# A batched matrix product in 32-row groups: which engine waits for the stores at the end

## The chip, the cores and the metric

The kernel runs on one core of one Trainium2 chip. A core has a matrix engine (TensorE, PE in the profile), a vector engine (VectorE, DVE), a scalar engine (ScalarE, ACT), a general engine (GpSimd, POOL) and an engine that issues transfers and waits (SyncE, SP). Each has its own stream of instructions; they meet only at semaphores. Transfers between the chip's main memory and the on-chip memory are done by 16 DMA engines. The metric is the time of one execution on the device in microseconds (us); less is better.

## The reference

```python
x: float32 [32, 256, 512]      # batch, i, j
y: float32 [32, 512, 384]      # batch, j, k
out = np.einsum('bij,bjk->bik', x, y).astype(np.float32)   # [32, 256, 384]
```

For each of 32 batches, a 256 x 512 matrix times a 512 x 384 matrix. 41.94 MB are read and 12.58 MB written.

## The kernel before, in words

The work is cut into N = 8 steps of Q = 4 batches. The 128 partitions of the on-chip memory are four groups of 32, one batch to a group. In a step each partition holds 8 rows of x (`x_sb`, 2,048 KB for the step) and 16 rows of y (`y_sb`, 3,072 KB), both double-buffered.

The engines share a step like this:

- SyncE issues all transfers, on one queue. It loads y and x of the first two steps ahead of everything else; later loads wait until GpSimd has cast the tile that they overwrite (L98 to L102). Then it issues three stores by `store` (L93 to L96): steps 0 to 4 together, steps 5 and 6 together, and step 7. Each store raises semaphore `s_out` by 16 when it has landed.
- GpSimd casts x and y from float32 to float16 (`round_x`, L121; `round_y`, L130).
- VectorE transposes x in 32 x 32 blocks, two float16 numbers at a time (`transpose_x`, L156), so that j comes to lie on the partitions.
- TensorE forms the products, in 16 slices of j with 32 rows each, the four batches side by side in the array (L217), and sums them in the accumulators `o_ps`.
- ScalarE copies 11 and VectorE 5 of every 16 blocks of the accumulators to `o_sb`, which holds the whole output (`collect`, L165).

The order on each engine is the order in which the program is written; semaphores hold it. SyncE's end is L107 to L111: it waits until ScalarE and VectorE have copied the last blocks, issues the last store, raises `s_sp` by 1, and then waits at L111 until `s_out` has reached 48, that is until all three stores have landed, and subtracts 48 so that the next execution starts from zero. Raising `s_sp` tells GpSimd that SyncE has no more waits on any other semaphore. GpSimd, whose casts are long done, waits for that (L144) and then clears the 24 semaphores of the kernel in one instruction (L145). `s_out` is the one semaphore that stands outside the cleared range; it has the next number, 123, and the range ends with `s_sp`, 122.

Of the kernel before, what the change touches and what calls it, by code (L numbers as in the profile page):

```python
# [19 lines left out]
def kernel(  # L20
# [41 lines left out]
    s_out = nc.alloc_semaphore("s_out")  # L62
# [28 lines left out]
    sp = nc.sync  # L91
# [16 lines left out]
    sp.wait_ge(s_dve, NE)  # L108
    store(N - 1, N)
    sp.sem_inc(s_sp, 1)  # L110
    sp.wait_op(s_out, 16 * 3, "sem-ge").then_inc(s_out, -16 * 3)  # L111

# [4 lines left out]
    po = nc.gpsimd  # L119
# [23 lines left out]
        round_y(n)  # L143
    po.wait_ge(s_sp, 1)  # L144
    po.sem_clear(range(nums[0], nums[-1] + 1))  # L145

# [132 lines left out]
```

## Time and profile before

| | |
|---|---|
| time, median of 3 runs | 132.00 us (131.89 to 132.18) |
| profiled execution | 132.13 us |
| its span, first to last instruction of the kernel | 130.8 us |
| busy: TensorE, VectorE, ScalarE, GpSimd | 61.4, 82.7, 84.1, 74.2 us |
| DMA queue, share of 16 engines | 98.1% |
| landing of the three stores after their issue | 33.9, 17.3, 11.5 us |

The span is shorter than the time of the same execution, because the time holds more than the kernel's own instructions. In the page, "L111" is line 111 of the kernel, a queue name with a q (SPq, POOLq) is an engine's sequencer, which waits, branches and issues without the engine counting as busy, and "a <- b" in a list of waits says that a waited for b. Rows of groups give the number of instructions after an x, and the duration in ns as least, median and most. A row of the timeline begins with the start and the length in us.

### The profile page before, as it was taken

What the parts mean: (1) busy time and instruction counts of PE and PEld (TensorE: products, weight loads), DVE (VectorE), ACT (ScalarE), POOL (GpSimd) and SP (SyncE); (2) the same over time, 40 slices, a digit from 0 to 9 for tenths busy, and PEclk for the clock granted to TensorE, in tenths of its full rate; (3) what the DMA queues carried; (4) which work ended last, traced back from release to release, by engine and by line L of the source; (5) the groups of instructions that cost most, each with busy time, mean ns of one, the idle gap of its engine ahead of it and who ended that gap; (6) DMA issues with size and microseconds to landing.
All of it is one profiled execution on the core that took longest, in us unless ns stands there. A gap on an engine that the chain in (4) does not pass through costs nothing. (4 is left out here: it accounts for less than half of the span.)

```text
span 130.8 us, 3199 instructions
## 1 busy us (share of the span) xinstructions
PE 61.4 (47%) x1024; PEld 46.7 (36%) x1024; DVE 82.7 (63%) x144; ACT 84.1 (64%) x178; POOL 74.2 (57%) x42
## 2 busy tenths in 40 slices
PE   0000009910992589089329905980975499100000
PEld 0000009800991566046129604970953236000000
DVE  0000036899379999985997997599999957920000
ACT  0400000599659989993998899399999957994000
POOL 0006991199929965992899459758973970000000
PEclk9999999995589689977986985599599959965555
DMA  5999999999999999999999999999999999999995
GB/s 120 451 396 441 421 431 451 443 408 428 451 413 421 438 443 401 436 436 443 423 458 398 443 408 466 398 418 436 463 398 408 427 438 425 436 428 421 425 440 248
DMA packets 3379, 54.55 MB, mean 417 GB/s; under 512 B 304, under 2 KB 304, under 8 KB 304
## 3 DMA queue, kind: packets, MB, share of 16 engines
q1 hardware_dynamic: 3376, 54.53, 98.1%
q14 instruction: 3, 0.02, 0.0%
HBM read 41.94 MB, written 12.58 MB: 417 GB/s over the span
## 5 line engine op out<-in xcount | busy, mean ns | idle before, releaser
L165 ACT COPY o_sb<-o_ps (+1 forms) x176 | 82.6, 469 | 31.7 <-PE o_ps L217 29.6
L217 PE MATMUL o_ps<-y_r,xt_sb 32*128 32x384 f16 x1024 | 61.4, 384 | 50.4 <-PEq L214 49.5
L217 PEld LDWEIGHTS o_ps<-y_r,xt_sb 32*128 32x128 f16 x1024 | 46.7, 107 | 64.6 <-issue 56.8
L156 DVE STREAM_TRANSPOSE xt_sb<-x_r 128x256 f32<-128x256 f32 x64 | 38.1, 626 | 30.9 <-POOL x_r L126 18.4
L136 POOL CAST y_r<-y_sb 128x1536 f16<-128x1536 f32 (+1 forms) x22 | 44.3, 2049 | 15.8 <-DMA y_sb<-in_y_dram 15.3
L165 DVE COPY o_sb<-o_ps 32x384 f32 (+1 forms) x80 | 44.6, 557 | 1.6
L126 POOL CAST x_r<-x_sb 128x2048 f16<-128x2048 f32 x16 | 30.2, 1893 | 16.8 <-DVE o_sb L165 12.1
L202 ACT ACT_TABLE_LOAD x1 | 1.3, 1283 | 3.4 <-PEq L78 3.4
L265 POOL MEMSET const-float32-0.0<- 128x1 f32 x1 | 0.1, 98 | 0.2 <-issue 0.2
L202 ACT COPY spare<-const-float32-0.0 1x1 f32<-1x1 f32 x1 | 0.2, 190 | 0.0
L265 POOL MEMSET const-bfloat16-1.0<- 128x1 bf16 x1 | 0.1, 101 | 0.0
L265 POOL MEMSET const-uint8-127<- 128x1 uint8 x1 | 0.1, 101 | 0.0
L265 POOL MEMSET const-float32-1.0<- 128x1 f32 x1 | 0.1, 98 | 0.0
## 6 DMA issues: line engine op xcount, KB each, us to landing
y_sb<-in_y_dram SPq DMA_DIRECT2D x8, 3072.0 KB, 16.8
x_sb<-in_x_dram SPq DMA_DIRECT2D x8, 2048.0 KB, 17.0
out_dram<-o_sb SPq DMA_DIRECT2D x1, 7680.0 KB, 33.9
out_dram<-o_sb SPq DMA_DIRECT2D x1, 3072.0 KB, 17.3
out_dram<-o_sb SPq DMA_DIRECT2D x1, 1536.0 KB, 11.5
```

The lines of the kernel that those rows point to most:

```text
L126: po.tensor_copy(x_r[:, e], x_sb[n % 2][:, e * H : (e + 1) * H]).then_inc(s_cast, 1)
L136: ins = po.tensor_copy(y_r[:, s], y_sb[n % 2][:, s])
L156: v.transpose(xt_w[:, w], words[:, e, w]).then_inc(s_xt, 1)
L165: ins = copy(o_sb[g * PQ : (g + 1) * PQ, n, e, h], o_ps[h * PQ : (h + 1) * PQ, e * Q + g, :K],)
L202: a_.copy(spare, nc.const_aps.tensor(0.0, [1, 1], F32))
L217: return te.add_instruction(mybir.InstMatmult(name=nc.get_next_instruction_name(), start_tensor_calc=start, stop_tensor_calc=stop, tile_si ...
L265: nc = _bacc.Bacc("TRN2", target_bir_lowering=False, num_devices=1)
```

## The change

The last instruction of SyncE, the wait for the three stores with its subtraction, is taken from SyncE's stream and put at the end of GpSimd's stream, behind the clear. SyncE's last instruction is then the raising of `s_sp`. Everything else is the same.

```diff
     sp.wait_ge(s_dve, NE)
     store(N - 1, N)
     sp.sem_inc(s_sp, 1)
-    sp.wait_op(s_out, 16 * 3, "sem-ge").then_inc(s_out, -16 * 3)
...
     po.wait_ge(s_sp, 1)
     po.sem_clear(range(nums[0], nums[-1] + 1))
+    po.wait_op(s_out, 16 * 3, "sem-ge").then_inc(s_out, -16 * 3)
```

## The prediction

> **What bounds the kernel now.** I read the page first, the slices in time and the DMA queue before anything else, because the edit touches nothing but the waiting for transfers.
>
> ```profile
> span 130.8 us, 3199 instructions
> PE 61.4 (47%) x1024; PEld 46.7 (36%) x1024; DVE 82.7 (63%) x144; ACT 84.1 (64%) x178; POOL 74.2 (57%) x42
> DMA  5999999999999999999999999999999999999995
> q1 hardware_dynamic: 3376, 54.53, 98.1%
> ```
>
> No engine is busy for two thirds of the span, while the 16 DMA engines are busy in every slice and for 98.1% of it. The kernel is a stream of 54.53 MB on SyncE's queue with all computing under it. Neither the bytes nor the moments at which a transfer is issued are changed, so the only stretch in which the edit can act is the end. That end stands in the stage table (columns: stretch, its length, each engine's busy time and instructions, clock, DMA share, GB/s), the waits of SyncE's queue, and the timeline of the last microseconds.
>
> ```profile
> core 0: us, PE busy (x) PEld busy (x) DVE busy (x) ACT busy (x) POOL busy (x), PEclk, DMA share, GB/s
> 112.00:119.90 7.90, 0.00 (x0) 0.00 (x0) 3.09 (x6) 7.06 (x16) 0.00 (x0) 0.70 1.01 431
> 119.90:130.80 10.90, 0.00 (x0) 0.00 (x0) 0.00 (x0) 0.00 (x0) 0.00 (x0) 0.50 0.87 373
> ...
> SPq L111 <- SPq L111: 11.1, 1, 11.1
> ...
> 109.44 5.73 DVE L165 COPY o_sb<-o_ps 32x384 f32<-32x384 f32 x10
> ...
> 117.82 1.43 ACT L165 COPY o_sb<-o_ps 32x384 f32<-32x384 f32 x3
> 119.27 0.34 SPq L96 DMA_DIRECT2D out_dram<-o_sb  x1
> ...
> L145 POOLq EVENT_SEMAPHORE_RANGE_CLEAR  x1: 163/163/163, 119.7 to 119.7; - x1
> L111 SPq EVENT_SEMAPHORE  x1: 17/17/17, 130.8 to 130.8; - x1
> ```
>
> TensorE is done before 112.0, VectorE at 109.44 + 5.73 = 115.17, ScalarE at 117.82 + 1.43 = 119.25. SyncE issues the last store at 119.27, GpSimd clears semaphores at 119.7, and from 119.9 on nothing runs but the stores. SyncE waits 11.1 us for them at L111 and its 17 ns at 130.8 are the end of the span.
>
> **What lies behind the span.** The profiled execution took 132.13 us, the span is 130.8, so 1.33 us lie around it. No view shows instructions there, but the trace also records the time of each update of each semaphore, and these go on. Semaphore 2 belongs to no instruction of this kernel. Its updates, and three others on which I draw, from that record (not a view; us from the span's start):
>
> ```
> semaphore 2, ahead of the span:  -0.371 -0.337 -0.298 -0.254 -0.231 -0.119 -0.081 -0.047 0.000
> semaphore 2, end of the kernel:  111.912 119.360 120.402 120.446 130.937 130.981 131.020 131.054 131.101
> semaphore 2, after the clears:   131.895 131.929 131.967 132.011 132.035 132.133 132.171 132.206 132.252
> semaphore 123 (s_out):           last arrival 130.767, subtracted by SyncE 130.801
> semaphore 96 (start of program): last arrivals 2.893 and 3.221, subtracted by GpSimd 2.942 and 3.270
> semaphore 97 (start of program): raised by GpSimd 3.021, subtracted by SyncE 3.055
> semaphore 122 (s_sp):            cleared by GpSimd 119.838 (the last of its range)
> ```
>
> It always comes in groups of nine: a chain through five engines and back. The group at the end tells the order, set beside the ends above: 111.912 is TensorE, 119.360 ScalarE (0.11 behind its last copy), 120.402 GpSimd, 120.446 VectorE (long done, so only 0.044 behind the one ahead), 130.937 SyncE, and then four steps back through the same engines to 131.101. From 131.063 to 131.671 nearly all semaphores of the core are reset, and the third group follows. So every engine passes the chain after its last instruction of the kernel, and whoever comes last holds it up.
>
> **The change, part by part.** (1) Removed: SyncE's wait and subtraction. Nothing is queued behind it on SyncE, and no instruction of the kernel waits for SyncE after s_sp. SyncE is then done at about 119.7 and is ready in the chain 11 us early. Gain by itself: the end no longer holds SyncE's wake-up (130.767 to 130.801, 0.034) and its way into the chain (130.801 to 130.937, 0.136).
>
> (2) Added: the same wait, one instruction, on GpSimd, behind the range clear. It moves past no DMA: GpSimd issues none, and SyncE's three stores are all issued before. Nothing is queued behind it. The clear stays at 119.7, covered by the stores as now; were that cover gone it would cost its 163 ns. The instruction itself is priced by the barriers at the start of the program, where both engines execute the same kind:
>
> ```profile
> L78 POOLq EVENT_SEMAPHORE  x4: 17/17/17, 2.9 to 3.3; - x4
> L78 SPq EVENT_SEMAPHORE  x2: 17/17/17, 3.0 to 3.4; - x2
> L78 POOLq DRAIN  x2: 34/38/41, 0.7 to 3.1; - x2
> L78 SPq DRAIN  x3: 7/7/123, 2.7 to 3.1; - x3
> L265 POOLq DRAIN  x1: 188/188/188, 0.3 to 0.3; - x1
> ```
>
> 17 ns on both. From arrival to subtraction GpSimd took 49 ns (2.893 to 2.942, and 3.221 to 3.270), SyncE 34 (3.021 to 3.055, and the same at the end). So GpSimd subtracts at 130.767 + 0.049 = 130.816, 15 ns later than SyncE does now.
>
> (3) GpSimd's way from its last instruction into the chain. It starts at 119.7 with 163 ns, by the record's finer times until 119.865, and the chain shows it at 120.402: 0.537 us. No other engine needed that: ScalarE 0.11, SyncE 0.136. Today it lies under 10 us of stores and costs nothing; after the edit it is the last thing on the path. What it consists of, no row shows. It could belong to the range clear (a tail of that instruction), and then it stays covered, because the clear still runs at 119.7. It could belong to GpSimd's leaving the kernel, and then it moves to the end. Two things in the record favour the second. In the reset after the chain the last clear of semaphores 105 to 154, by the order of the engines GpSimd's share, is at 131.444, and GpSimd had no delay in the group that follows: its step at 131.967 is 0.038 behind ScalarE's, as in the group ahead of the span (0.039). It was thus ready at most 0.485 after a clear, against 0.564 (119.838 to 120.402) at the kernel's end. And TensorE, which resets last (131.671), is back in the chain 0.224 later, so a reset need not have a tail of half a microsecond. I take 0.537. Lower end: 0.11, ScalarE's; 0 is excluded by the fastest engine seen. Upper end: 0.537 + 0.188, the longest GpSimd drain in the rows.
>
> (4) GpSimd's place in the chain. SyncE is the turning point: after its step four more follow, 131.101 - 130.937 = 0.164. GpSimd is third, so six follow: 0.298 in the group ahead of the span (-0.298 to 0.000), 0.285 in the last. VectorE and SyncE are ready by then and add only their steps. I take 0.298.
>
> **The sum**, from the last arrival at 130.767. Before: 0.034 + 0.136 + 0.164 = 0.334, the chain closes at 131.101. After: 0.049 + 0.537 + 0.298 = 0.884, it closes at 131.651. Difference +0.550 us. The reset and the last group follow the closing, so I carry the difference over in full: the profiled execution would take 132.13 + 0.55 = 132.68. It stands 0.13 above the median of the runs, 132.00, so I forecast 132.55 us, 0.42% slower. With the ends of (3): 0.049 + 0.11 + 0.298 - 0.334 = +0.12, and 0.55 + 0.188 = +0.74.
>
> A measurement of this kernel can tell about 0.2%, 0.26 us, from no change; its three runs span 131.89 to 132.18.
>
> **Rivals.** *Only the place counts.* GpSimd leaves the kernel like the others, the 0.537 was the clear's tail. For it: the clear is the only kind of instruction in the kernel's end that no other engine executes; against it: the 0.485 above. With SyncE's 0.136 the sum is 0.049 + 0.136 + 0.298 - 0.334 = +0.15, with ScalarE's 0.11 it is +0.12: 132.12 to 132.15, not to be told from no change.
>
> The Trainium skill, Runtime: NRT & Kernel Launch, in its section on the preamble and postamble, describes this chain as a serpentine over five engines with 44 ns a hop, eight hops in about 355 ns. The trace agrees: 131.895 to 132.252 is 0.357. By that rule alone an engine that comes last costs by its place only, and as an estimate two more hops make 0.088 us, a time of 132.09. It has no term for an engine that is slow to leave, and that term is what decides here.
>
> *Faster.* SyncE leaves the kernel 11.1 us early (its row above), and whatever SyncE does for its own queue at the end would be done under the stores. Place: from 130.801 on, and in what follows the third group, which nothing shows. Of the visible part only 0.034 + 0.136 can go, and the same steps of GpSimd take its place; with GpSimd's six steps at 0.298 the closing would be earlier only if its wake-up and leaving together took under 0.334 - 0.298 = 0.036, less than its wake-up alone. For a gain beyond 0.26 the hidden part would have to hold some 0.4 us of SyncE's own work against the +0.12 that is left at the least: 131.7. The 1.33 around the span leave room for that, no row speaks for it.
>
> *The edit does not reach the time.* If the end of the measured time is not tied to this chain (it is taken at the span's end, plus something fixed), only the 15 ns of wake-up remain: 132.02.
>
> **How the numbers follow.** Slow leaving moved to the end, 132.55: 0.65. Only the place, 132.12 to 132.15: 0.23. Not in the measured time, 132.02: 0.07. Faster, 131.7: 0.05. So slower 0.65, the same 0.30, faster 0.05. The likeliest case has 132.35 to 132.80 for itself: its upper end of +0.74 and the spread of the runs, and below it a leaving partly owed to the clear. The range for 8 in 10 takes in the place-only case and reaches from 132.0 to 132.8; the faster case and half of the one at 132.02 lie beneath it.
>
> **What would show it.** The span should grow by no more than 0.02: GpSimd's subtraction with 17 ns at 130.8 in place of SyncE's, the 11.1 us of waiting gone from L111, the clear still at 119.7, the three stores issued and landing as before. In the record of semaphore 2, SyncE no longer makes the late step: the third update, GpSimd's, comes some 0.54 behind its subtraction, and six steps in 0.3 us follow. A third update only 0.11 to 0.15 behind the subtraction proves the first rival right. The prediction is wrong as a whole if the time moves by over 0.3 us while the chain closes as early as before, or if a store's landing moves.

## The result, and the profile after

The changed kernel takes 132.51 us (median of 6 runs, 132.41 to 132.65); the kernel before took 131.97 in its 6 runs (131.83 to 132.18). The ratio is 1.0038, with a 95% interval of 1.0028 to 1.0048: 0.5 us slower, a small change but one clear of the spread of the runs.

The page of the changed kernel, its DMA lines, two windows at the end (columns: stretch, its length, each engine's busy time and instructions, clock, DMA share, GB/s), all waits of SyncE's queue, and the rows of GpSimd's last two lines and of SyncE's last store:

```profile
span 130.6 us, 3199 instructions
DMA  5999999999999999999999999999999999999996
q1 hardware_dynamic: 3376, 54.53, 98.3%
...
112.00:119.50 7.50, 0.00 (x0) 0.00 (x0) 2.68 (x5) 6.67 (x15) 0.00 (x0) 0.84 1.00 426
119.50:130.60 11.10, 0.00 (x0) 0.00 (x0) 0.00 (x0) 0.00 (x0) 0.00 (x0) 0.50 0.90 384
...
SPq L73 <- POOL x_r L125: 42.4, 6, 7.8
SPq L69 <- POOL x_r L125: 34.4, 6, 16.7
SPq L96 <- PE o_ps L217: 25.1, 2, 23.4
SPq L108 <- DVE o_sb L165: 4.5, 1, 4.5
SPq L96 <- ACT o_sb L165: 4.1, 1, 4.1
SPq L265 <- PEq L265: 0.7, 1, 0.7
SPq L78 <- PEq L78: 0.4, 2, 0.3
...
118.87 0.34 SPq L96 DMA_DIRECT2D out_dram<-o_sb  x1
...
L144 POOLq EVENT_SEMAPHORE_RANGE_CLEAR  x1: 161/161/161, 119.3 to 119.3; - x1
L145 POOLq EVENT_SEMAPHORE  x1: 17/17/17, 130.6 to 130.6; - x1
```

The stream of transfers is what it was. The wait of 11.1 us is gone from SyncE's list, and the last instruction, 17 ns, is now GpSimd's, at 130.6. The span is 0.2 us *shorter* than the 130.8 before, and yet the execution took longer: 132.51 against 132.13. So the loss is wholly outside the kernel's own instructions: 1.9 us lie around the span in place of 1.3. That is so in every run and not only in the profiled one: the time less the span (on record to 0.1) is 1.91 to 1.95 in the six runs of the changed kernel, and 1.29 to 1.41 in the runs of the kernel before that were taken beside the experiments. The span is shorter because the last store landed earlier in this execution, at 130.588 and not 130.767; the spans of the kernel before themselves range from 130.4 to 131.5 over its runs, so a difference of 0.2 says nothing of the change.

What follows the span is again in the trace's record of semaphore updates (not a view), here of semaphore 2, the closing chain, and of `s_out`, in us from the span's start:

```
                     before                                   after
last store landed    130.767                                  130.588
subtracted           130.801 (SyncE)                          130.637 (GpSimd)
TensorE, ScalarE     111.912 119.360                          111.989 118.961
GpSimd               120.402                                  131.195
VectorE, SyncE       120.446 130.937                          131.239 131.263
back to TensorE      130.981 131.020 131.054 131.101          131.360 131.399 131.433 131.479
landing to closing   0.334                                    0.891
time - closing       132.13 - 131.101 = 1.029                 132.51 - 131.479 = 1.031
```

The chain closes 0.891 behind the landing, 0.557 later than before, and the time lies 1.03 behind the closing in both, if it is counted from the span's start. Where the measured time itself begins and ends, no record shows; that the difference stays the same is what matters here.

### The profile page after: what moved, and what is told of

Its sections match the earlier page's. It is cut to its first block, busy times and chain, and to the rows that moved or that the text cites. A ratio compares the mean times of both kernels' runs of the same rounds, so it can differ in the third digit from the quotient of the medians.

```text
span 130.6 us, 3199 instructions
## 1 busy us (share of the span) xinstructions
PE 63.6 (49%) x1024; PEld 49.2 (38%) x1024; DVE 82.5 (63%) x144; ACT 84.3 (64%) x178; POOL 74.1 (57%) x42
## 5 line engine op out<-in xcount | busy, mean ns | idle before, releaser
L217 PE MATMUL o_ps<-y_r,xt_sb 32*128 32x384 f16 x1024 | 63.6, 391 | 48.2 <-PEq L214 48.1
L217 PEld LDWEIGHTS o_ps<-y_r,xt_sb 32*128 32x128 f16 x1024 | 49.2, 110 | 62.2 <-issue 54.9
```

The source lines that it names most:

```text
L217: return te.add_instruction(mybir.InstMatmult(name=nc.get_next_instruction_name(), start_tensor_calc=start, stop_tensor_calc=stop, tile_si ...
```

## The experiments

The theory: every engine passes the chain when it has left the kernel, and the last to come sets the time by its wake-up, its way into the chain and the steps behind its place; GpSimd's way is half a microsecond, any other engine's far less. The rivals: it was the place or the parting from SyncE that cost; or a state in which GpSimd stood, from the range clear, from unsettled work or from long idling.

In the table and the texts below "wake-up" runs from the last landing to the subtraction of `s_out`, "way" from there to the engine's step in the chain, and "steps" from there to the closing, all in us and from the record of semaphore updates.

**ScalarE waits, and VectorE waits.** Against the changed kernel:

```diff
-    po.wait_op(s_out, 16 * 3, "sem-ge").then_inc(s_out, -16 * 3)
...
+    a_.wait_op(s_out, 16 * 3, "sem-ge").then_inc(s_out, -16 * 3)
```

The second kernel has `v` for `a_`; either line stands at the end of its engine's stream.

> The wait for the stores is ScalarE's last instruction. Theory 1 (GpSimd alone is slow to leave the kernel; any other engine pays its wake-up, its own way into the chain and the steps behind its place): wake-up 0.045 (semaphore 97 raised 3.021, subtracted by ScalarE 3.066), way 0.114 (last copy to its step), seven steps 0.336, together 0.495 against SyncE's 0.334, so +0.16 us: 132.13. Rival (any engine but SyncE pays about half a microsecond, because SyncE's early leaving or the long sleep is what costs): +0.55, 132.5.

> The wait for the stores is VectorE's last instruction. Theory 1: wake-up 0.057 (3.021 to 3.078 in the barrier at the start), a way of 0.11 to 0.14 like ScalarE's and SyncE's, five steps 0.254: 0.42 to 0.45 against 0.334, +0.09 to +0.12 us, 132.06 to 132.09. Rival (any engine but SyncE pays half a microsecond): 132.5.

**TensorE waits**, in the same way, with `te`.

> The wait for the stores is TensorE's last instruction, at the first place of the chain. Theory 1 (wake-up, own way, steps behind the place; only GpSimd's way is long): wake-up 0.091 (3.021 to 3.112), way 0.16 or a little more (TensorE's last product to its step), eight steps 0.371, together 0.62 to 0.66 behind the landing against SyncE's 0.334: +0.29 to +0.33 us, 132.25 to 132.3. By place alone it would be the dearest of all engines and stand above GpSimd's +0.56.

The rows of the waiting instruction in these three kernels, ScalarE, VectorE and TensorE (whose semaphore instructions the profile lists under its weight loads, PEld):

```profile
L210 ACTq EVENT_SEMAPHORE  x1: 17/17/17, 130.6 to 130.6; - x1
```

```profile
L192 DVEq EVENT_SEMAPHORE  x1: 21/21/21, 130.9 to 130.9; - x1
```

```profile
L251 PEldq EVENT_SEMAPHORE  x1: 51/51/51, 130.5 to 130.5; - x1
```

Each is the last instruction of its span. Beside them the two kernels from above, in the order of the chain:

| waits | wake-up | way | steps | sum | + over SyncE's | measured median | ratio, 95% interval |
|---|---|---|---|---|---|---|---|
| TensorE | 0.091 | 0.223 | 0.359 | 0.673 | 0.339 | 132.28 | 1.0029 (1.0008 to 1.0049) |
| ScalarE | 0.045 | 0.142 | 0.325 | 0.512 | 0.178 | 132.15 | 1.0012 (0.9999 to 1.0024) |
| GpSimd | 0.049 | 0.558 | 0.284 | 0.891 | 0.557 | 132.51 | 1.0038 (1.0028 to 1.0048) |
| VectorE | 0.057 | 0.185 | 0.250 | 0.492 | 0.158 | 132.25 | 1.0027 (1.0012 to 1.0043) |
| SyncE | 0.034 | 0.136 | 0.164 | 0.334 | 0 | 131.97 | 1 |

ScalarE came out within 0.02 of what was expected by its time, and TensorE within the range given for it. The rival that any engine but SyncE pays half a microsecond falls: those with a long sleep of 11 us and more pay 0.16 to 0.34. The place counts too, 0.164 to 0.359 over the five places, but it does not order the engines: GpSimd stands in the middle and is the dearest, by its way alone. VectorE's median of 132.25 missed the expected 132.06 to 132.09. Its way was 0.185, not 0.11 to 0.14, and its runs scatter from 131.93 to 132.96; the chain's +0.158 is a ratio of 1.0012, the lower end of the interval.

The chain was read in one execution of each kernel, but the time less the span can be formed for every run. Its mean is 1.34 with SyncE waiting, 1.47 with VectorE, 1.52 with ScalarE, 1.62 with TensorE and 1.92 with GpSimd: the order of the sums in the table, here from all runs. (TensorE's stands a little less above SyncE's than its sum does, because its longer wake-up and its 51 ns of instruction lie within the span.) For VectorE it settles where the rest of the median lies. Only 0.13 us of it is behind the span; its spans are longer, 130.8 in the median against 130.6 for the kernel before, and they scatter from 130.4 to 131.5. As the kernel before has spans up to 131.5 too, this can be chance in the stream of transfers; what makes a span long stays open.

**A drain ahead of the wait.**

```diff
     po.sem_clear(range(nums[0], nums[-1] + 1))
+    po.drain()
     po.wait_op(s_out, 16 * 3, "sem-ge").then_inc(s_out, -16 * 3)
```

> GpSimd waits for the stores, with a drain of GpSimd between its clear and that wait. Theory 1 (the 0.56 lies in GpSimd's way out, behind its last instruction): as without the drain, third update 0.54 to 0.56 behind the subtraction, 132.5. Rival (GpSimd still has earlier work to settle, which a drain under the stores would settle): the way shrinks to 0.11 to 0.15, 132.12.

GpSimd's clear, its drain and its wait, each from the view of its line:

```profile
L144 POOLq EVENT_SEMAPHORE_RANGE_CLEAR  x1: 161/161/161, 120.0 to 120.0; - x1
...
L145 POOLq DRAIN  x1: 34/34/34, 120.2 to 120.2; - x1
```

The drain finds nothing to settle: 34 ns, as in the barriers at the start. The time is 132.57 (ratio 1.0051, 1.0038 to 1.0064), wake-up 0.050, way 0.558, steps 0.287. The record of instructions has the clear from 119.986 to 120.147 and the drain from 120.181, so GpSimd goes on 0.034 after the clear: the clear has no tail of half a microsecond that would hold up GpSimd's next instruction.

**SyncE clears, GpSimd waits; SyncE clears and waits.**

```diff
-    sp.sem_inc(s_sp, 1)
+    sp.wait_ge(s_sp, 1)
+    sp.sem_clear(range(nums[0], nums[-1] + 1))
...
-    po.wait_ge(s_sp, 1)
-    po.sem_clear(range(nums[0], nums[-1] + 1))
+    po.sem_inc(s_sp, 1)
```

In the first kernel GpSimd then waits for the stores, in the second SyncE does, as its last instruction.

> SyncE executes the range clear (once GpSimd has raised s_sp) and GpSimd, which clears nothing, waits for the stores as its last instruction. Theory 1: 132.5, third update 0.54 to 0.56 behind the subtraction. Rival (a range clear on GpSimd leaves it slow to leave, whenever it ran): the way is 0.11 to 0.15, 132.12.

> SyncE executes the range clear and then waits for the stores; GpSimd ends with raising s_sp. Theory 1: GpSimd's way out is covered, the chain closes 0.33 behind the landing, 131.95 as in the kernel before. If it mattered which engine executes the clear, the time would move.

The first of the two kernels, SyncE's clear and GpSimd's wait:

```profile
L111 SPq EVENT_SEMAPHORE_RANGE_CLEAR  x1: 72/72/72, 119.8 to 119.8; - x1
...
L145 POOLq EVENT_SEMAPHORE  x1: 17/17/17, 130.7 to 130.7; - x1
```

With no clear on GpSimd at all its way is 0.554 and the time 132.41 (ratio 1.0038, 1.0025 to 1.0051). With SyncE waiting, wake-up, way and steps are 0.034, 0.136 and 0.163, and the time is 131.95 (0.9993, 0.9977 to 1.0010). So where the clear is executed makes no difference that can be told; the engine that waits last makes all of it.

**More instructions on GpSimd behind the wait.**

```diff
     po.wait_op(s_out, 16 * 3, "sem-ge").then_inc(s_out, -16 * 3)
+    for _ in range(10):
+        po.sem_inc(s_out, 1)
+    po.wait_op(s_out, 10, "sem-ge").then_inc(s_out, -10)
```

> As the changed kernel, with eleven more semaphore instructions on GpSimd behind its wait (ten that raise s_out by 1, one that waits for 10 and subtracts them). Theory 1: GpSimd is alone on the path, so every one of them delays the third update one for one, its way of 0.55 to 0.56 begins behind the last of them, and the time grows by 0.2 to 0.9 us over 132.5 (17 ns is the instruction, 78 ns is the distance of two at the start of the program). If GpSimd's way ran in parallel to its last instructions, the way would shrink by what they take and the time stay at 132.5.

The added lines:

```profile
L147 POOLq EVENT_SEMAPHORE  x10: 17/17/17, 130.8 to 131.5; - x10
...
L148 POOLq EVENT_SEMAPHORE  x1: 17/17/17, 131.6 to 131.6; - x1
```

In the record of instructions the ten start 78 ns apart (130.800, 130.878, 130.956 and so on to 131.505), though each is shown with 17. From the first subtraction (130.741) to the second (131.625) they take 0.884, the way behind them is 0.554, the steps 0.286. The time is 133.37 (ratio 1.0105, 1.0088 to 1.0122), 0.86 over the changed kernel for 0.88 of instructions. They go one for one into the time, and the way starts behind the last of them; nothing of it runs beside them.

**A write by GpSimd's cores behind the wait.**

```diff
     po.wait_op(s_out, 16 * 3, "sem-ge").then_inc(s_out, -16 * 3)
+    po.memset(spare, 0.0)
```

> As the changed kernel, with a write of one element by GpSimd's cores behind the wait for the stores (the rows at the start show such a write with 98 to 102 ns). Theory 1, the way out as a fixed sequence behind the last instruction: the way is 0.55 to 0.56 from the end of that write, 132.6 to 132.65. If the way out is slow because GpSimd's cores have been idle for 20 us and must be woken, a write just ahead wakes them: the way behind it is 0.11 to 0.2 and the time 132.3 or less.

The end of the timeline:

```profile
119.47 0.34 SPq L96 DMA_DIRECT2D out_dram<-o_sb  x1
131.30 0.09 POOL L146 MEMSET spare<- 1x1 f32 x1 [23.61 <-POOLq L145]
```

The write ends 0.190 behind the subtraction, and GpSimd's step comes 0.513 after it (131.393 to 131.906). The time is 132.65 (ratio 1.0052, 1.0036 to 1.0069), 0.14 over the changed kernel. With its cores at work just before, after 23.61 us of rest, GpSimd leaves hardly faster: 0.513, where a fixed way had been expected at 0.55 to 0.56 and a way shortened by the waking at 0.11 to 0.2. Idling of the cores isn't the reason; the 0.04 by which the way is shorter stays open.

No kernel tried beats the one before: SyncE has the shortest wake-up, the shortest way and the fewest steps behind it.

## Why the prediction was right

- **The part of the path.** Predicted: 132.55, +0.550. Measured: 132.51, +0.54 between the medians, +0.557 in the chain. The likeliest case, given 0.65, held by its mechanism and not only by its number, and the first rival (place only, 132.12 to 132.15) fell by its own test: GpSimd's step came 0.558 behind its subtraction, not 0.11 to 0.15.
- **Part 2, the instruction.** Forecast 17 ns, and 49 ns from landing to subtraction; both came out so. That the barriers at the start of this program price a wait at its end held for all five engines: 34, 45, 49, 57 and 91 ns.
- **Part 3, the way.** Taken at 0.537, measured 0.558, 0.558, 0.554 and 0.554 in the four kernels where a semaphore instruction is GpSimd's last. Its attribution was the real risk. The argument from the resets (0.485 against 0.564) was weak, because it only bounds the delay behind a clear at 0.485 and so left nearly all of the 0.54 undecided: that it pointed the right way was in part luck. The drain beginning 0.034 after the clear, and the kernel with no clear on GpSimd, show it directly. The upper end, a drain of 0.188, had no ground in what was measured: the drain of the idle GpSimd took 34 ns.
- **Part 4, the place.** Six steps were put at 0.298 and took 0.284. This error and the 0.021 of the way partly cancel, so the sum is nearer than its terms.
- **Part 1, the gain from SyncE.** SyncE was ready early and added only its step (131.239 to 131.263). No hidden work of SyncE's appeared: the time stands 1.03 behind the closing before and after, and 1.03 to 1.07 in the other eight kernels. That also settles the rival by which the change would not reach the time.
- **The span.** It was to grow by no more than 0.02; it shrank by 0.2, because the last landing moved by 0.18 between two executions. The instruction itself moved as forecast (15 ns between the wake-ups); the statement should have been made from the landing, not from the span's start. For the same reason "if a store's landing moves" was no usable sign of being wrong: the landing did move, by less than the spans of one and the same kernel differ from run to run.

The Trainium skill, Runtime: NRT & Kernel Launch, in its section on the preamble and postamble, gives 44 ns a hop and eight hops for this chain, in the row of the preamble. The trace agrees for the closing chain as a whole: eight steps took 0.359 in the kernel with TensorE last. By hops alone, as an estimate from that figure, the change would have cost 0.09.

It cost 0.56 in the chain: 0.015 in the wake-up, 0.422 in the way and 0.120 in the place (0.284 against 0.164). So the engine's own way is the main part. The place, too, is not a count of equal steps: behind GpSimd's the six are 0.044, 0.024, 0.097, 0.039, 0.034 and 0.046.

## What to carry to other kernels

What the last instruction of a kernel costs depends on the engine that executes it, even when it is one wait of 17 ns. In this kernel the engine that leaves fastest, SyncE, should wait for the final stores, and GpSimd should finish at least half a microsecond ahead of the end. A span that doesn't grow says nothing of such a change: compare the execution's time with the span, and read what happens after the last instruction from the semaphores. A delay that is covered today (GpSimd's 0.54 under 10 us of stores) has to be priced before work is moved behind the cover.

## What was not expected of the hardware

- GpSimd needs 0.51 to 0.56 us from its last instruction to its step in the closing chain, against 0.136 (SyncE), 0.142 (ScalarE), 0.185 (VectorE) and 0.223 (TensorE). That it was slower was read off beforehand; that a drain, the clear's absence and fresh work on its cores change it by at most 0.05 was not. What GpSimd does in that time, no record shows, and it stays open.
- Semaphore instructions of GpSimd follow each other at 78 ns, though their rows show 17. Two at the start of the program had shown this distance; that ten in a row keep it, and that the time pays for it in full, is what the run with the added instructions showed.
- A range clear of the same 24 semaphores takes 161 to 163 ns on GpSimd and 72 on SyncE.
